# Where one projection of a dilated attention is computed: beside the values by block products, or in the attention's slots

## The chip, the cores and the metric

The kernel runs on one core of a Trainium2 chip. The metric is the device time of one execution in microseconds; the median of three runs is compared. One further execution was profiled, and the profile below is of that one.

## The reference

Two layers of a decoder on x of 1024 positions by 1024 features, in float32. Layer 0 mixes positions by a gated MLP, layer 1 by attention with three dilations; each is followed by a squared-ReLU MLP. The change touches the attention alone:

```python
B_PATTERNS = ((128, 1), (512, 4), (2048, 16))
def dilated_branch(q, k, v, window, dilation, slopes):
    span = window // dilation                                   # 128 in all three
    # positions in blocks of span x dilation; a query sees the keys of its own residue,
    # in its own block and in the one before
    s = jnp.einsum('bnqrhe,bnkrhe->bnrhqk', qb, kb) * (E ** -0.5)
    s = s + bias;  s = jnp.where(valid, s, NEG)                 # ALiBi, causal, within span
    m = jnp.max(s, axis=-1);  p = jnp.exp(s - m);  l = jnp.sum(p, axis=-1)
    o = jnp.einsum('bnrhqk,bnkrhe->bnqrhe', p / l, vb);  lse = m + jnp.log(l)
def mixer_b(h, w_qkv, w_out, slopes):
    qkv = (h @ w_qkv).reshape(B, S, N_PAT, 3, B_HEADS, B_HEAD_DIM)   # 16 heads of 64
    wts = softmax(lses over the patterns);  o = sum(wts * outs)
    return o.reshape(B, S, 1024) @ w_out
```

So nine projections of 1024 x 1024 (q, k and v for three dilations) come ahead of the attention proper.

## The kernel before

[...]

**The product stage** (`values`). v of all three dilations and q and k of dilation 1 are made by a scheme of seven products of half-size blocks in place of eight: `V_STEPS` lists (pattern g, X, product p) with X = 0 for q, 1 for k, 2 for v. A product has four blocks m of 128 rows; each is 12 matmuls 512 wide (`psv`, line 1283). `evict` takes the sums of a block out of PSUM: products 1, 5 and 6 are copied to `vpart`, the others add what was kept, split it into `vs` or `qs`, and GpSimd's queue stores that in DRAM (`v_dram`, `qk_dram`), 512 KB a block. Right-hand blocks of the weights come by `RightForms.load` (512 KB each) and are prepared two steps ahead.

**The attention stage** (`attention`). The 8 pairs of heads are taken in turn, and in each pair dilation 16, then 4, then 1 (`order`; g = 2, 1, 0). Each of these 24 units has 8 slots of two halves. `at(slot, half, rank)` and `in_half(half_slot, rank)` put pieces of work into a half slot; the loop at the end runs all half slots in order and puts projection steps between them. In a unit:

- `scores`: three matmuls a tile into `sc`, both heads at once (line 1473); `soften`: DVE adds the bias and takes the extreme (line 1493), ACT makes exponent and sum (line 1495), into `p`.
- `transposes` of `p` into `pT`; `halve` splits it into `pThi` (ACT) and `pTlo` (DVE); three half slots later `weighted` multiplies by v into `pv`, two banks of 512 positions.
- `gather`: for each of the two banks ACT copies one half of the sums into `oT` (line 1562) and DVE adds the other (line 1563).
- `merge`, for the three dilations of a pair: factors from the sums, and `scale`, `add`, `cut` on DVE (lines 1649 to 1653).

PSUM has two banks each for `sc`, `pv`, the transposes and the projections.

**Projections in the slots** (`project`). q and k of dilations 16 and 4, 8 pairs: 32 items of 128 columns, each two halves of 24 matmuls (`psq`, `psk`, line 1384), whose weights come by one load of 512 KB and are split (`wqk_hi`, `wqk_lo`). A step of the stream is 3 matmuls, so an item has 16 steps and there are 512. `lead` steps run ahead of the first half slot, the rest by a running credit:

```python
stream = project()
lead, credit = 7 * KD, 0
...
credit += 512 - lead
while credit >= 351:
    credit -= 351
    next(stream, None)
```

That is 1.3 steps a half slot, done after 351 of the 384. Blocks of q and k of dilation 1 are loaded by `load_block`, v by `load_v`, on SP's queue. The order on each engine is fixed when the kernel is built; a scheduler may move an instruction, above all a load, ahead of where the code stands. Near the end the slots also take the first part of the output product (`pso`, line 1756).

Of the kernel before, what the change touches and what calls it, by code (L numbers as in the profile page):

```python
# [10 lines left out]
F32 = mybir.dt.float32  # L11
# [6 lines left out]
P = 128  # L18
# [17 lines left out]
def trunk(ctx: ExitStack, tc: tile.TileContext, x, c, ada_w, ada_b, ln_g, ln_b, a_w_in, a_b_in,  # L36
# [1063 lines left out]
    qk_dram = dram.tile([N_PAIRS, 2, P, 2, S], F32, name="qk_0")  # L1100

# [43 lines left out]
    V_STEPS = [(g, X, p) for g, X in ((2, 2), (1, 2), (0, 2), (0, 0), (0, 1)) for p in (1, 2, 5, 6, 7, 4, 3)]  # L1145
# [11 lines left out]
    def values(before, right, ahead):  # L1157
# [3 lines left out]
        with ExitStack() as ph:  # L1161
# [79 lines left out]
            def evict(g, X, p, m):  # L1241
                acc = sums["pb" if p in (2, 5, 3) else "pa", m][:]
                if p in (1, 5, 6):
                    t = parts[p, m] = x_tile(f"vpart_{g}_{X}_{p}_{m}")
                    A.copy(t[:], acc)
                    return
                if p != 4:
                    t = parts.pop(({2: 1, 7: 5, 3: 6}[p], m))
                    V.tensor_tensor(t[:], acc, t[:], op=ALU.add)
                    acc = t[:]  # L1250
                half, dh = {2: (1, 0), 3: (1, 1), 4: (0, 0), 7: (0, 1)}[p]
                if X < 2:
                    t = parted.tile([P, 2, HALF], F32R, name=f"qs_{X}_{p}_{m}", tag="vs")
# [44 lines left out]
    def attention(form):  # L1298
# [5 lines left out]
        with ExitStack() as ph:  # L1304
# [104 lines left out]
            def attend(n, oT_of):  # L1409
# [21 lines left out]
                heads = [dict(probs={}, pvs=[], begun=[False, False]) for _ in range(2)]  # L1431
# [17 lines left out]
                if g == 0:  # L1449
                    for m, slot in enumerate((base - 4, base - 3, base + starts[0] + 1, base + starts[1] + 1)):  # L1450
                        at(slot, 0)(lambda m=m: load_block(m))

                def scores(m):
# [10 lines left out]
                    for t in groups[m]:  # L1464
# [4 lines left out]
                        tq, keys = slice(t * P - q_from, (t + 1) * P - q_from), slice(k0 - k_from, k0 - k_from + w)  # L1469
# [28 lines left out]
                for m, slot in enumerate(starts):  # L1498
                    at(base + slot, 0, 1)(lambda m=m: scores(m))
                    for part in range(2):  # L1500
                        at(base + slot, part, 3)(lambda m=m, part=part: soften(m, part))

                for e, st in enumerate(heads):
# [36 lines left out]
                    def weighted(m, e=e, h=h, rows=rows, packs=packs, pT=pT, pvs=pvs, st=st):  # L1540
                        if m == 0:
                            pvs.extend(bank("pv", f"pv_{h}_{g}_{b}") for b in range(2))
                        begun, left = st["begun"], st["left"]
                        for t, nxt, o in packs[m]:
                            stt = my["v"][:, t, 2 * e : 2 * e + 2, :].rearrange("p a c -> p (a c)")
                            for x_ in pT[m]:
# [3 lines left out]
                                for q0, o_, w_ in pieces:  # L1550
                                    b = q0 // HALF
                                    left[b] -= 1
# [4 lines left out]
                    def gather(e=e, rows=rows, pvs=pvs):  # L1557
# [298 lines left out]
```

## Time and profile before

| | |
|---|---|
| median of three runs | 2716.02 us (2713.87 to 2716.73) |
| profiled execution, its own time | 2714.54 us |
| its span, first to last instruction | 2712.8 us |
| mean granted clock of TensorE | 0.996 |
| product stage / ahead of the first score / slots up to the last projection | 386.3 / 38.4 / 539.3 us |
| last slots / output sums | 63.0 / 72.0 us |
| matmuls | 13242 |
| HBM read / written | 365.40 / 136.92 MB |

PE is TensorE's matmuls, PEld its weight loads, DVE VectorE, ACT ScalarE, POOL GpSimd, SP the engine that issues most transfers. A row of a group gives line, engine, operation, output<-input, shapes, count, then busy time and mean duration in ns, then the idle time of the engine just before and what ended it. A row of waits gives total, number of times and the longest. In the chain of waits a piece has its start, its length and what ran. Buffer numbers are left out of names, and lines are those of the kernel before.

### The profile page before, as it was taken

To read this page: it belongs to the slowest core of one execution; us is meant where nothing else is said; L and a number is where in the kernel's file an instruction comes from. 1 tells how busy PE (TensorE), PEld (TensorE's weight loads), DVE (VectorE), ACT (ScalarE), POOL (GpSimd) and SP (SyncE) were. 2 spreads that over 40 slices of the span, in tenths; PEclk is the share of its full clock that TensorE was granted. 3 is DMA by queue.
4 is the path that set the end of the run, shared out by engine and by line. 5 is a ranking of instruction groups with operands and counts; after the bars stand their busy time and mean duration, and the time that the engine had idled before them with its cause. 6 is when DMAs were issued, how large, how long until landed. Compare 5 with 4: busy or idle time off the path is not lost.

```text
span 2712.8 us, 37098 instructions
## 1 busy us (share of the span) xinstructions
PE 2652.8 (98%) x13242; PEld 2193.6 (81%) x13242; DVE 1993.4 (73%) x3610; ACT 1378.9 (51%) x2601; POOL 114.6 (4%) x193
## 2 busy tenths in 40 slices
PE   6999999999999999999999999999999999999998
PEld 5788888887888877888888888888877888878887
DVE  6787698877889778655647777777658966577877
ACT  3354375555444464443436666666645655554332
POOL 1000000000000001111111000000010000000000
PEclk9999999999999999999999999999999999999999
DMA  7534336667967745655475545554782654485562
GB/s 265 159 119 134 117 133 225 229 219 251 337 224 248 245 150 178 215 184 195 165 226 171 138 137 136 138 146 135 232 222 96 210 189 160 148 312 189 172 208 86
DMA packets 340781, 504.77 MB, mean 186 GB/s; under 512 B 51900, under 2 KB 177252, under 8 KB 340596
## 3 DMA queue, kind: packets, MB, share of 16 engines
q1 hardware_dynamic: 324212, 443.68, 51.4%
q0 software_dynamic: 16384, 58.73, 6.0%
q8 instruction: 104, 1.70, 0.3%
q14 instruction: 81, 0.66, 0.1%
HBM read 365.40 MB, written 136.92 MB: 185 GB/s over the span
## 4 chain that ended last, share of the span: by engine, by line
PE 82%; DVE 10%; DMA 4%; ACT 2%; issue 2%; SPq 0%; DVEq 0%; POOL 0%; ACTq 0%; POOLq 0%
PE psd L957 22%; PE psv L1283 13%; PE psua L798 9%; PE psk L1384 7%; PE psq L1384 7%; PE psuc L798 4%; PE pv L1553 3%; PE psd_wout L389 3%; PE psu L368 3%; PE sc L1473 3%; PE psub L798 2%; DMA adaw<-in_ada_w_dram 2%; PE psv L470 2%; PE pT L1526 1%; DVE left L103 1%
## 5 line engine op out<-in xcount | busy, mean ns | idle before, releaser
L798 PE MATMUL psua<-right,left 128*128 128x512 f32 x1536 | 363.2, 390 | 0.1
L957 PE MATMUL psd<-rhi,lhi 128*128 128x512 f32 x896 | 350.1, 391 | 3.0 <-ACT part L829 3.0
L957 PE MATMUL psd<-rlo,lhi 128*128 128x512 f32 x896 | 349.8, 390 | 0.2
L957 PE MATMUL psd<-rhi,llo 128*128 128x512 f32 x896 | 349.3, 390 | 0.0
L798 PEld LDWEIGHTS psua<-right,left 128*128 128x128 f32 x1536 | 287.3, 188 | 61.1 <-DVE right L103 1.2
L1495 ACT ACTIVATE p<-p,stat 128x128 f32<-128x128 f32 (+1 forms) x384 | 168.8, 441 | 95.4 <-DVE stat L1493 94.4
L957 PEld LDWEIGHTS psd<-rhi,lhi 128*128 128x128 f32 x896 | 168.6, 188 | 39.0 <-ACT part L829 3.9
L957 PEld LDWEIGHTS psd<-rlo,lhi 128*128 128x128 f32 x896 | 168.7, 188 | 35.7 <-DVE rlo L103 1.1
L957 PEld LDWEIGHTS psd<-rhi,llo 128*128 128x128 f32 x896 | 168.7, 188 | 35.0
L798 PE MATMUL psuc<-right,left 128*128 128x512 f32 x768 | 187.2, 391 | 0.0
L128 DVE SCALAR_TENSOR_TENSOR adaacc<-adaw,silu_c,adaacc 128x512 f32<-128x512 f32 x168 | 128.7, 776 | 55.7 <-DMA adaw<-in_ada_w_dram 55.0
L798 PEld LDWEIGHTS psuc<-right,left 128*128 128x128 f32 x768 | 143.6, 188 | 29.8 <-DVE right L103 0.2
L103 DVE TENSOR_TENSOR pTlo<-pT,pThi 128x512 fp32r<-128x512 f32 (+1 forms) x160 | 99.3, 621 | 76.0 <-ACT pThi L102 75.0
L103 DVE TENSOR_TENSOR left<-ws,left 128x512 fp32r<-128x512 f32 x128 | 88.0, 689 | 73.9 <-ACT left L102 72.0
L103 DVE TENSOR_TENSOR llo<-lraw,lhi 128x1024 fp32r<-128x1024 f32 x112 | 136.7, 1221 | 1.5 <-ACT lhi L102 1.5
L102 ACT CAST left<-ws 128x512 fp32r<-128x512 f32 x128 | 79.1, 620 | 98.3 <-DVE ws L719 88.5
L1384 PE MATMUL psk<-form_L,wqk_hi 128*128 128x512 f32 x384 | 127.0, 412 | 0.0
L1384 PE MATMUL psq<-form_L,wqk_hi 128*128 128x512 f32 x384 | 126.5, 410 | 0.0
L102 ACT CAST lhi<-lraw 128x1024 fp32r<-128x1024 f32 x112 | 117.2, 1047 | 9.3 <-PE psd L957 3.3
L1283 PE MATMUL psv<-vrhi,form_S 128*128 128x512 f32 x384 | 120.0, 391 | 0.8 <-ACT vrhi L102 0.5
L1493 DVE CUSTOM_DVE_ANT_0 p<-sc,bias 128x128 f32<-128x128 f32 (+1 forms) x384 | 113.7, 346 | 5.6 <-PE sc L1473 5.3
L102 ACT CAST pThi<-pT 128x512 fp32r<-128x512 f32 (+1 forms) x160 | 84.7, 529 | 62.1 <-PE pT L1526 45.3
(332 smaller groups left out, 6076.6 us busy)
## 6 DMA issues: line engine op xcount, KB each, us to landing
lraw<-forms SPq DMA_DIRECT2D x112, 512.0 KB
adaw<-in_ada_w_dram SPq DMA_DIRECT2D x192, 256.0 KB
up<-in_mlp_w_up_dram SPq DMA_DIRECT2D x64, 512.0 KB
forms<-s SPq DMA_DIRECT2D x128, 256.0 KB
rraw<-in_mlp_w_down_dram SPq DMA_DIRECT2D x64, 512.0 KB
forms<-part SPq DMA_DIRECT2D x96, 256.0 KB
v<-vs POOLq DMA_DIRECT2D x48, 512.0 KB, 3.9
vraw<-in_b_w_qkv_dram SPq DMA_DIRECT2D x42, 512.0 KB
```

The source lines that it names most:

```text
L102: first = A.copy(hi, src) if hi_engine is A else hi_engine.tensor_copy(hi, src)
L103: return first, lo_engine.tensor_tensor(lo, src, hi, op=ALU.subtract)
L128: ins = V.scalar_tensor_tensor(acc[:], raw[:], silu_c[:, k : k + 1], acc[:], ALU.mult, ALU.add)
L368: T.matmul(dst, s[a], m[b], start=(n == 0), stop=(n == last))
L389: T.matmul(p[:], stat[a][:, k, o : o + P], u[b][:, w], start=n == 0, stop=n == count - 1)
L798: T.matmul(acc, w[:, a, k, :], right[p][:, b, k, :], start=p in (1, 2, 5) and k + a + b == 0, stop=k == 3 and a == 1, skip_group_check=True)
L957: ins = T.matmul(sums[kind, m][:], l[a][:, k, m * P : (m + 1) * P], r[b][:, k, :], start=p in (1, 5, 2, 3) and kp + k + a + b == 0, stop=k ...
L1283: T.matmul(acc, rows[:, m * P : (m + 1) * P], cols_, start=p in (1, 2, 5) and kp + k + a + b == 0, stop=kp == 1 and k == 1 and a == 1, ski ...
L1384: T.matmul(p[:], wu[a][:, k * P : (k + 1) * P], h_op(k, half, b), start=k + c_ == 0, stop=k == KD - 1 and c_ == 2)
L1473: T.matmul(banks[e][:, sl], q_[a][rows, tq], k_[b][rows, keys], start=c_ == 0, stop=c_ == 2)
L1493: V.tensor_tensor_reduce(out=pr, in0=banks[e][:, sl], in1=st["bias"][:, width - w :], scale=-0.125, scalar=3e38, op0=ALU.add, op1=ALU.min, ...
L1495: A.activation(pr, pr, AF.Exp, bias=nm, scale=-1.0, accum_out=l)
```

## The change

Four things are changed.

- **q of dilation 4 moves.** `V_STEPS` gets the seven products of (1, 0), between v and the q of dilation 1. Its evictions read PSUM with a stride of 4, so that positions stand by residue, and store to `q1_dram`, one store of 512 KB a block. `project` has 24 items (384 steps) instead of 32; in its place `load_q` reads the two halves of a pair's q, 512 KB each, on SP's queue.
- **The lead and the pace.** 40 steps ahead instead of 56; then 328 steps over the first 326 half slots, and 16 over the rest up to 351.
- **Sums bank by bank.** `gather` copies a bank when its last product is done, and `join`, the add, stands a half slot later. A bank of `pv` is taken at its first use. The two row operations on `aff` stand a half slot apart, too.
- **Starts** are given in half slots, and the fourth of dilation 1 moves from 12 to 11.

```diff
-    V_STEPS = [(g, X, p) for g, X in ((2, 2), (1, 2), (0, 2), (0, 0), (0, 1)) for p in (1, 2, 5, 6, 7, 4, 3)]
+    V_STEPS = [(g, X, p) for g, X in ((2, 2), (1, 2), (0, 2), (1, 0), (0, 0), (0, 1)) for p in (1, 2, 5, 6, 7, 4, 3)]
...
+                def side(t):
+                    return t.rearrange("p (r i) -> p r i", r=4) if (g, X) == (1, 0) else t
+                if (g, X) == (1, 0):
+                    acc = acc.rearrange("p (i r) -> p r i", r=4)
...
-                    A.copy(t[:], acc)
+                    A.copy(side(t[:]), acc)
...
-                    V.tensor_tensor(t[:], acc, t[:], op=ALU.add)
+                    V.tensor_tensor(side(t[:]), acc, side(t[:]), op=ALU.add)
...
-                    split(t[:, 0], t[:, 1], acc)
-                    nc.gpsimd.dma_start(qk_dram[4 * dh + m, X, :, :, half * HALF : (half + 1) * HALF], t[:].bitcast(F32))
+                    split(side(t[:, 0]), side(t[:, 1]), acc)
+                    dst = q1_dram[4 * dh + m] if g else qk_dram[4 * dh + m, X]
+                    nc.gpsimd.dma_start(dst[:, :, half * HALF : (half + 1) * HALF], t[:].bitcast(F32))
...
-                todo = [(n, X) for n in range(len(order)) if order[n][1] for X in range(2)]
+                todo = [(n, X) for n in range(len(order)) for X in {0: (), 1: (1,), 2: (0, 1)}[order[n][1]]]
...
-                starts = {0: (0, 2, 3, 5) if last_one else (0, 2, 4, 6), 1: (0, 2, 5), 2: (0, 4)}[g]
+                starts = {0: (0, 4, 6, 10) if last_one else (0, 4, 8, 11), 1: (0, 4, 10), 2: (0, 8)}[g]
+                @at(max(0, base - 8), 0)
+                def load_q():
+                    if g != 1:
+                        return
+                    for i, m in enumerate(("qhi", "qlo")):
+                        my[m] = qk[1].tile([P, S], F32R, name=f"{m}_{hp}_1", tag=m)
+                        nc.sync.dma_start(my[m][:].bitcast(F32), q1_dram[hp, :, i, :])
...
-                        tq, keys = slice(t * P - q_from, (t + 1) * P - q_from), slice(k0 - k_from, k0 - k_from + w)
+                        q0 = (t % 2 * 4 + t // 2) * P if g == 1 else t * P - q_from
+                        tq, keys = slice(q0, q0 + P), slice(k0 - k_from, k0 - k_from + w)
...
-                        for b in range(2):
-                            dst = oT[rows, b * HALF : (b + 1) * HALF]
-                            A.copy(dst, pvs[b][rest, :])
-                            V.tensor_tensor(dst, dst, pvs[b][main, :], op=ALU.add)
+                    def gather(b, e=e, rows=rows, pvs=pvs, rest=rest):
+                        dst = oT_of(e, b)[rows, b * HALF : (b + 1) * HALF]
+                        A.copy(dst, pvs[b][rest, :])
+                    def join(b, e=e, rows=rows, pvs=pvs, main=main):
+                        dst = oT_of(1)[rows, b * HALF : (b + 1) * HALF]
+                        V.tensor_tensor(dst, dst, pvs[b][main, :], op=ALU.add)
...
-                    in_half(then + (not last_one), 2)(gather)
+                        for b in range(2):
+                            if m == ((1, 3) if g < 2 else (0, 1))[b]:
+                                done_at = then + (not last_one or b == 0)
+                                in_half(done_at, 2)(lambda b=b, f=gather: f(b))
+                                in_half(done_at + 1, 2)(lambda b=b, f=join: f(b))
...
-            lead, credit = 7 * KD, 0
+            lead, credit = 5 * KD, 0
...
-                    credit += 512 - lead
-                    while credit >= 351:
-                        credit -= 351
+                    credit += (368 - lead) * 25 if 2 * n + half_of < 326 else 16 * 326
+                    while credit >= 326 * 25:
+                        credit -= 326 * 25
```

What this does to the order of instructions is shown at three places. First PE, in the unit of dilation 16 of the fourth pair (heads 6 and 7), from the transposes of head 6's first pack (`pT_6_2_0`) to its first products with v (`pv_6_2_0`). Before:

```order
L1526 MATMUL pT_6_2_0_14644<-ident_73,p_6_2_0_14414 128x128 x2
L1526 MATMUL pT_6_2_0_14644<-ident_73,p_6_2_2_14431 128x128 x2
L1384 MATMUL psq_4_2_1_14633<-form_L11_8184,wqk_16_hi_14351 128x512 x2
L1384 MATMUL psq_4_2_1_14633<-form_L11_8184,wqk_16_lo_14352 128x512
L1384 MATMUL psq_4_2_1_14633<-form_L11_8184,wqk_16_hi_14351 128x512 x2
L1384 MATMUL psq_4_2_1_14633<-form_L11_8184,wqk_16_lo_14352 128x512
L1384 MATMUL psq_4_2_1_14633<-form_L12_8185,wqk_16_hi_14351 128x512 x2
L1384 MATMUL psq_4_2_1_14633<-form_L12_8185,wqk_16_lo_14352 128x512
L1384 MATMUL psq_4_2_1_14633<-form_L12_8185,wqk_16_hi_14351 128x512 x2
L1384 MATMUL psq_4_2_1_14633<-form_L12_8185,wqk_16_lo_14352 128x512
L1553 MATMUL pv_6_2_0_14672<-pThi_6_2_0_14653,v_3_2_14348 128x128
L1553 MATMUL pv_6_2_0_14672<-pTlo_6_2_0_14654,v_3_2_14348 128x128
```

The same place now:

```order
L1543 MATMUL pT_6_2_0_14953<-ident_73,p_6_2_0_14730 128x128 x2
L1543 MATMUL pT_6_2_0_14953<-ident_73,p_6_2_2_14753 128x128 x2
L1392 MATMUL psq_4_2_1_14912<-form_L12_8186,wqk_12_hi_14562 128x512 x2
L1392 MATMUL psq_4_2_1_14912<-form_L12_8186,wqk_12_lo_14563 128x512
L1392 MATMUL psq_4_2_1_14912<-form_L12_8186,wqk_12_hi_14562 128x512 x2
L1392 MATMUL psq_4_2_1_14912<-form_L12_8186,wqk_12_lo_14563 128x512
L1392 MATMUL psq_4_2_1_14912<-form_L12_8186,wqk_12_hi_14562 128x512 x2
L1392 MATMUL psq_4_2_1_14912<-form_L12_8186,wqk_12_lo_14563 128x512
L1570 MATMUL pv_6_2_0_14976<-pThi_6_2_0_14959,v_3_2_14671 128x128
L1570 MATMUL pv_6_2_0_14976<-pTlo_6_2_0_14960,v_3_2_14671 128x128
```

Nine projection matmuls stand between the transposes and their use, where twelve stood.

Second DVE at the same place, up to the low part of that pack (`pTlo_6_2_0`); `oT_2_0` are the sums of the pair before. Before:

```order
L103 TENSOR_TENSOR klo_3_1_14358<-psk_3_1_0_14491,khi_3_1_14357 128x4x128
L103 TENSOR_TENSOR wqk_19_lo_15058<-wk_4_1_raw_14629,wqk_19_hi_15057 128x1024
L1563 TENSOR_TENSOR oT_2_0_14482<-oT_2_0_14482,pv_5_0_1_14496 64x512
L103 TENSOR_TENSOR pTlo_6_2_0_14654<-pT_6_2_0_14644,pThi_6_2_0_14653 128x512
L1563 TENSOR_TENSOR oT_3_2_14785<-oT_3_2_14785,pv_6_2_0_14672 64x512
```

Now:

```order
L1649 RECIPROCAL mal_2_14893<-mal_2_14893 128x16
L1651 TENSOR_TENSOR ma_2_14888<-ma_2_14888,mal_2_14893 128x16 x3
L1582 TENSOR_TENSOR oT_2_0_14724<-oT_2_0_14724,pv_5_0_1_14831 64x512
L103 TENSOR_TENSOR pTlo_6_2_0_14960<-pT_6_2_0_14953,pThi_6_2_0_14959 128x512
L1582 TENSOR_TENSOR oT_3_2_15020<-oT_3_2_15020,pv_6_2_0_14976 64x512
```

The low parts of a key half and of a weight no longer stand ahead of `pTlo` there; small operations of `merge` do.

Third SP's queue, around the load of v for dilation 1 of the fifth pair (`v_4_0`); `mst` and `st_dram` carry the sums for `merge`, `bq` and `bk` are the blocks of dilation 1. Before:

```order
L1361 DMA wk_6_2_raw_16041<-in_b_w_qkv_dram 128x8x128
L1608 DMA mst_4_16348<-st_dram_11367 128x4x8
L1361 DMA wq_6_1_raw_16302<-in_b_w_qkv_dram 128x8x128
L1423 DMA v_4_0_15908<-v_0_108 128x8x256
L1588 DMA st_dram_11367<-stat_4_1_15633 128x8x4
L1608 DMA mst_4_16348<-st_dram_11367 128x4x8
L1441 DMA bq_4_2_15984<-qk_0_111 128x2x256
L1441 DMA bk_4_2_15986<-qk_0_111 128x2x384
```

Now:

```order
L1369 DMA wq_7_2_raw_16620<-in_b_w_qkv_dram 128x8x128
L1450 DMA qhi_5_1_16520<-q_1_112 128x1024
L1450 DMA qlo_5_1_16522<-q_1_112 128x1024
L1431 DMA v_4_0_16145<-v_0_108 128x8x256
L1611 DMA st_dram_11900<-stat_4_1_15887 128x8x4
L1631 DMA mst_4_16566<-st_dram_11900 128x4x8
L1457 DMA bq_4_2_16224<-qk_0_111 128x2x256
L1457 DMA bk_4_2_16226<-qk_0_111 128x2x384
```

The two loads of the next pair's q stand ahead of `v_4_0` and of the blocks, where the weight of q of dilation 4 stood.

More of the change, by code (lines that the diff above doesn't have):

```diff
@@ L1100, in trunk @@
     qk_dram = dram.tile([N_PAIRS, 2, P, 2, S], F32, name="qk_0")
+    q1_dram = dram.tile([N_PAIRS, P, 2, S], F32, name="q_1")
     class RightForms:
@@ L1551, in weighted @@
                                     b = q0 // HALF
+                                    if b not in pvs:
+                                        pvs[b] = bank("pv", f"pv_{h}_{g}_{b}")
                                     left[b] -= 1
```

35 lines of the change are left out of this document (16 added, 19 removed).

## The prediction

> **What bounds the kernel now.** I read the page first, then the table of windows over the stages that the change touches, the chain of waits there, and PE's waits. The page: PE is busy in 98% of the span, and PE matmuls make 82% of the chain that ends last.
>
> ```profile
> PE 2652.8 (98%) x13242; PEld 2193.6 (81%) x13242; DVE 1993.4 (73%) x3610; ACT 1378.9 (51%) x2601; POOL 114.6 (4%) x193
> PE 82%; DVE 10%; DMA 4%; ACT 2%; issue 2%; SPq 0%; DVEq 0%; POOL 0%; ACTq 0%; POOLq 0%
> ```
>
> Windows of the five stages in order: block products, projections ahead of the first score, slots up to the last projection, last slots, and the output sums (columns: length, PE, weight load, DVE, ACT, POOL, clock, DMA share, GB/s).
>
> ```profile
> 991.00:1377.30 386.30, 385.46 (x1714) 317.98 (x1713) 248.03 (x310) 171.28 (x244) 47.49 (x80) 1.00 0.57 197
> 1377.30:1415.70 38.40, 38.40 (x172) 31.54 (x170) 15.46 (x18) 10.12 (x14) 3.35 (x7) 1.00 0.75 232
> 1415.70:1955.00 539.30, 539.06 (x3650) 454.36 (x3651) 387.18 (x1190) 344.87 (x1034) 23.85 (x51) 1.00 0.53 149
> 1955.00:2018.00 63.00, 60.62 (x392) 50.42 (x391) 38.24 (x115) 41.06 (x113) 8.21 (x10) 1.00 0.93 238
> 2018.00:2090.00 72.00, 66.38 (x297) 53.56 (x297) 54.02 (x132) 27.90 (x43) 0.00 (x0) 0.95 0.41 130
> ```
>
> In the first three PE has no hole, and DVE (64%, 40%, 72%) and ACT have room. A full row of PE could hide waits, since matmuls overlap. So I take their price from the chain of waits in order of time (start, length, what, count):
>
> ```profile
> 1224.89 152.77 PE psv L1283 x674
> 1388.54 10.88 PE psk L1384 x48
> ...
> 1493.43 1.39 PE psk L1384 x6
> ...
> 1499.13 1.57 PE psq L1384 x6
> ...
> 1504.16 2.78 PE psq L1384 x12
> ```
>
> 152.77/674 and 10.88/48 are both 0.227 us per 512-wide matmul back to back. In the slots a run of 6 takes 1.39 and one of 12 takes 2.78, 0.232 each; behind a score burst the run of 6 takes 1.57, so a handover costs up to 0.18.
>
> [...] Priced by weight load (2193.6/13242 = 0.166 us each), the 48 matmuls that the change saves would be worth 8 us, against 11 by the chain's pitch.
>
> PE's weight loads waited in the slots (waits view, 1415 to 1930 us: total, times, longest):
>
> ```profile
> PEld sc L1473 <- issue: 9.0, 53, 0.4
> PEld pv L1553 <- DVE pTlo L103: 1.0, 4, 0.3
> PEld pT L1529 <- ACT p L1495: 0.7, 2, 0.4
> ```
>
> The first row is a cost of each score burst and stays. The others are the real waits for DVE and ACT, under 2 us in 515. PE's own work sets the time.
>
> **The change part by part.** The tile view of `psq`, PE alone, gives the projections of q, half of them for dilation 4:
>
> ```profile
> L1384 PE MATMUL psq<-form_L,wqk_hi x384: 387/393/506, 1377.5 to 1935.4; 128*128 128x512 f32 x192
> L1384 PE MATMUL psq<-form_L,wqk_lo x192: 387/393/401, 1378.0 to 1935.6; 128*128 128x512 f32 x192
> L1384 PE MATMUL psq<-form_S,wqk_hi x128: 387/393/502, 1382.9 to 1929.6; 128*128 128x512 f32 x128
> L1384 PE MATMUL psq<-form_S,wqk_lo x64: 389/393/398, 1383.4 to 1929.8; 128*128 128x512 f32 x64
> ```
>
> *Matmuls.* They sum to 768; 384 go. Seven products of 4 blocks with 12 matmuls each come: 336. Beside the values: 336 x 0.227 = +76.2 us. Ahead of the first score: the lead falls from 56 to 40 steps of 3, so 48 x 0.227 = -10.9. In the slots 336 go: -77.9 at 0.232. The instruction lists hold 284 projection runs between first score and last projection before and 278 after, so nearly all handovers stay: 6 x 0.18 = -1. Sum: **-13.6**. Bounds: if a slot matmul is worth no more than 0.227, -11.2 without the runs; if it is worth the mean of the two runs of 6 above, (1.39 + 1.57)/12 = 0.247, -17.7. I take 0.232, because runs of 6 and 12 give the same.
>
> *What the products bring beside PE.* Each product has the weight cuts, evictions and 512 KB stores that the products of q and k of dilation 1 have now, written to other rows of the tile. Their stretch is the first chain row: no hole in 152.77 us, although ACT there waits for landings (waits, 985 to 1385):
>
> ```profile
> ACT qs L102 <- DMA qk<-qs: 31.0, 14, 5.0
> ```
>
> 16 more stores add about 16 us of such waits, beside ACT's 171 of 386; I cost them at nothing. Without the cover, 0 to 16. The strided read of PSUM moves from the projection's cut to the eviction; if it were dearer there, DVE's 36% of room takes it.
>
> *Two queues.* The projection's weights of q (8 loads of 512 KB) become 12, and 16 loads of q itself come on SP's queue. Per pair of heads that is 0.5 MB more net in the slots: at 149 GB/s for a share of 0.53, full rate is 281, so 1.8 us of transfer; the share rises from 0.53 to about 0.62. In SP's order the two loads of q stand ahead of v and of the third and fourth q and k blocks of dilation 1, some 4 us of transfer in front of blocks wanted half a pattern later. Nothing. If the cover is gone it shows at the end, below.
>
> *Sums bank by bank.* The add waits half a slot behind ACT's copy, so DVE doesn't stand for it. Each bank is copied when its last product is done: the first frees earlier, the second's add comes half a slot later than now. The lists of DVE and ACT over one pair in the steady part (waits behind the bar):
>
> ```profile
> L103 DVE TENSOR_TENSOR pTlo<-pT,pThi 128x384 fp32r<-128x384 f32 (+1 forms) x20 | 12.4, 622 | 10.8 <-ACT pThi L102 10.5
> L1563 DVE TENSOR_TENSOR oT<-oT,pv 64x512 f32<-64x512 f32 x12 | 8.2, 684 | 5.3 <-ACT oT L1562 5.2
> ...
> L103 DVE TENSOR_TENSOR wqk_lo<-wq_raw,wqk_hi 128x1024 fp32r<-128x1024 f32 x3 | 3.7, 1225 | 0.8 <-ACT wqk_hi L102 0.6
> ...
> L103 DVE TENSOR_TENSOR qlo<-psq,qhi 128x512 fp32r<-128x512 f32 x3 | 2.1, 692 | 1.7 <-ACT qhi L102 1.7
> L102 ACT CAST pThi<-pT 128x384 fp32r<-128x384 f32 (+1 forms) x20 | 10.6, 528 | 8.0 <-PE pT L1526 5.7 <-PE pT L1529 2.1
> ```
>
> And the same pair's three patterns by windows:
>
> ```profile
> 1633.60:1657.60 24.00, 24.00 (x167) 20.43 (x166) 15.94 (x60) 14.37 (x47) 0.77 (x2) 1.00 0.29 79
> 1657.60:1681.80 24.20, 24.20 (x165) 20.43 (x163) 18.14 (x52) 15.38 (x46) 0.81 (x2) 1.00 0.59 131
> 1681.80:1707.70 25.90, 25.90 (x175) 21.54 (x174) 19.94 (x55) 18.81 (x51) 0.59 (x2) 1.00 0.64 199
> ```
>
> DVE works 54.0 of 74.1 us. It loses two `qlo` and one `wqk_lo`, 2.6, leaving 51.4; PE loses 42 x 0.232 = 9.7, leaving 64.4. DVE goes from 73 to 80%, with 13.0 us of room for what are now 20.1 us of waits. The 5.3 for `oT` should mostly go; of the 10.8 for `pTlo`, ACT itself waits 7.8 for PE's transposes, and that shrinks with PE. So DVE still fits, but with less cover.
>
> *New PE waits.* The tightest place is the first pack of dilation 16 (timeline):
>
> ```profile
> 1652.13 0.60 PE L1526 MATMUL pT<-ident,p 128*128 128x128 f32 x4
> 1652.81 1.22 DVE L103 TENSOR_TENSOR wqk_lo<-wk_raw,wqk_hi 128x1024 fp32r<-128x1024 f32 x1 [0.26 <-ACT wqk_hi L102]
> 1654.79 0.69 DVE L103 TENSOR_TENSOR pTlo<-pT,pThi 128x512 fp32r<-128x512 f32 x1
> 1655.54 0.19 PEld L1553 LDWEIGHTS pv<-pTlo,v 128*128 128x128 f32 x1 [0.23 <-DVE pTlo L103]
> ```
>
> Twelve projection matmuls cover transpose to use; nine will, 0.7 us less. If DVE came as late as here, 0.7 more in 8 pairs, 5.6 us. After, the `wqk_lo` of 1.22 no longer stands ahead of `pTlo` there, so it may be nothing. Other packs lose about as much cover but have more. I take 4 between 0 and 8.
>
> Total: -13.6 + 4 = **-9.6, say -9**. The profiled execution took 2714.5 (span 2712.8); the median of the runs is 1.5 above it. So 2705.5 for such an execution, and 2707 for the median. About 0.2%, 5.4 us, is what a measurement can tell from no change.
>
> **The rivals.**
>
> *Late transfers at the end* (0.17). In the last pair's first two patterns the DMA engines are full, and PE has waited for a block once:
>
> ```profile
> 1954.20:1980.50 26.30, 26.30 (x173) 22.15 (x172) 18.34 (x53) 16.33 (x50) 3.14 (x4) 1.00 1.03 300
> PE sc L1473 <- DMA bk<-qk: 1.3, 1, 1.3
> ```
>
> The pattern ahead of this window loses 30 projections, 7 us, of the time in which the same output weights and rows must land. For: the share of 1.03. Against: SP's new order issues some of these loads earlier. It gives back up to 7: -13.6 + 4 + 7 = -3, **2713**, no change.
>
> *DVE sets the pace* (0.13). In-order waits keep their length while the half slots shrink by a seventh. DVE's work and waits then set a pair: 51.4 + w against PE's 64.4. Slower by 5.4 needs 8 x (w - 13.0) above 19, so w above 15.4. For: without `oT` 14.8 of today's 20.1 are left, close to that. Against: 7.8 of these hang on PE itself. Halfway between 13.0 and 20.1, w = 16.5: 8 x 3.5 = +28, in place of the 4: -13.6 + 28 = +14, **2730**; all 20.1 would give +43.
>
> *Cheaper slots* (0.12). A removed slot matmul is worth 0.247 and nothing new waits: -17.7, **2698**.
>
> *The clock* (0.03). It was granted at 1.00 in the slots and 0.95 in the output sums, where PE stood idle 5.6 of 72 us: 0.05 x 72 = 3.6 us lost. If a late q or block holds PE some 4 us in one place, 4 + 3.6 beyond the sum give -2, **2714**. [...]
>
> That the change does not do what it says cannot be: the lists hold 48 matmuls fewer.
>
> **How the numbers follow.** The forecast has 0.55: PE stays the bound with 0 to 8 us of new waits, 2703 to 2711 around 2707. Its upper end touches the bound of 0.2%, so 0.50 of it counts as faster; with the cheaper slots 0.62. Slower: 0.13. The rest, 0.25, is within 0.2%. The range, 2697 to 2723, takes in cheaper slots, late transfers and the clock, and half the way to a pace by DVE; what is left out is most of DVE's 0.13 and a few hundredths below.
>
> **What would show it.** Right: seven products more at about 10.9 us each, the first score about 27 us behind the last product instead of 38, a steady pair of 64 to 66 us instead of 74, and PE's waits for `pTlo` in the slots below 8 us. Wrong: pairs of 67 us or more with DVE without idle time, PE waiting for `bk` or output weights at the end, or a clock below 1.00 in the slots. A product stage over 465 us would mean that its stores no longer hide.

## The result and the profile after

The changed kernel took 2724.9 us (median of 6 runs, 2721.8 to 2728.8) against 2716.2 for the kernel before: ratio 1.0036, 95% interval 1.0023 to 1.0049. It is slower by 0.36%, where 0.3% faster was forecast. The profiled execution's span went from 2712.8 to 2723.0.

The same five stages of the changed kernel, by windows (length, PE, weight load, DVE, ACT, POOL, clock, DMA share, GB/s):

```profile
990.00:1452.70 462.70, 461.54 (x2049) 381.09 (x2048) 291.86 (x360) 201.29 (x286) 57.84 (x96) 1.00 0.56 195
1452.70:1481.80 29.10, 27.79 (x122) 22.45 (x120) 10.68 (x14) 8.00 (x11) 3.25 (x6) 1.00 0.94 292
1481.80:1964.50 482.70, 468.70 (x3304) 391.52 (x3303) 370.20 (x1170) 328.91 (x1012) 25.44 (x52) 1.00 0.62 179
1964.50:2030.00 65.50, 64.40 (x401) 53.65 (x401) 39.18 (x115) 41.70 (x114) 8.19 (x10) 0.95 0.86 209
2030.00:2102.00 72.00, 66.37 (x297) 53.58 (x296) 54.28 (x133) 27.92 (x43) 0.00 (x0) 0.95 0.41 137
```

Against before the products took +76.4, the lead -9.3, the slots **-56.6**, the last slots +2.5 and the output sums 0; outside of these 2.8 went, 1.0 of it ahead of the products. The forecast for the slots was -77.9 - 1 + 4 = -74.9: all but a little of the miss is there. PE, which had no hole in the slots (539.06 of 539.30), now has 14.0 us of them.

What PE's weight loads waited for in lead and slots (waits view, 1452 to 1965 us: total, times, longest):

```profile
PEld sc L1490 <- issue: 8.9, 52, 0.4
PEld pv L1570 <- DVE pTlo L103: 8.7, 17, 0.7
PEld pv L1570 <- ACT pThi L102: 7.4, 11, 1.7
PEld sc L1490 <- DVE stat L1510: 6.2, 12, 1.0
PEld sc L1490 <- DVE aff L1726: 1.9, 2, 1.6
PEld psk L1392 <- DVE qlo L103: 1.7, 1, 1.7
```

The issue row is as before. Of the others, `psk` belongs to the lead; the rest, with two smaller rows of 0.8 and 0.2, are 25.2 us of waits in the slots. Before, such rows came to 3.7 us: the 1.7 of the two that the prediction shows, and 2.0 in six small ones that it leaves out. In the second to the sixth pair they come again at up to three places. The timeline at the first, the first pack of dilation 16:

```profile
1697.97 0.39 ACT L1512 ACTIVATE p<-p,stat 128x128 f32<-128x128 f32 x1
...
1698.48 0.58 ACT L1578 COPY oT<-pv 64x512 f32<-64x512 f32 x1
...
1699.08 0.59 ACT L102 CAST pThi<-pT 128x512 fp32r<-128x512 f32 x1
1699.09 0.69 DVE L1582 TENSOR_TENSOR oT<-oT,pv 64x512 f32<-64x512 f32 x1 [0.23 <-ACT oT L1578]
...
1699.72 0.19 PEld L1570 LDWEIGHTS pv<-pThi,v 128*128 128x128 f32 x1 [0.33 <-ACT pThi L102]
...
1699.81 0.69 DVE L103 TENSOR_TENSOR pTlo<-pT,pThi 128x512 fp32r<-128x512 f32 x1
...
1700.55 0.19 PEld L1570 LDWEIGHTS pv<-pTlo,v 128*128 128x128 f32 x1 [0.65 <-DVE pTlo L103]
```

ACT finishes the exponentials of the last burst and the previous pattern's copy of `oT` before it comes to `pThi`; DVE does the join before `pTlo`. PE has run through its nine projection matmuls and waits 0.33 and then 0.65. The second place is the second pack of dilation 4, with the same order ahead of it (waits of 0.79 and 0.62 in the pair before this one, 0.46 and 0.62 in this one). The third is the fourth score burst of dilation 1, moved from half slot 12 to 11, whose bank DVE has not read out yet (1.05 in the pair before). A steady pair takes 66.5 to 67.9 us from one such place to the next, not 74.1 and not the 64.4 of the forecast. One pair by windows:

```profile
1635.00:1702.70 67.70, 65.50 (x462) 54.74 (x461) 51.50 (x163) 46.11 (x141) 2.50 (x6) 1.00 0.59 163
```

DVE's groups in it (waits behind the bar), and ACT's:

```profile
L103 DVE TENSOR_TENSOR pTlo<-pT,pThi 128x512 fp32r<-128x512 f32 (+1 forms) x20 | 12.4, 620 | 6.6 <-ACT pThi L102 6.6
L1582 DVE TENSOR_TENSOR oT<-oT,pv 64x512 f32<-64x512 f32 x13 | 8.9, 684 | 8.7 <-ACT oT L1578 8.7
```

```profile
L1512 ACT ACTIVATE p<-p,stat 128x128 f32<-128x128 f32 (+1 forms) x48 | 21.1, 441 | 13.8 <-DVE stat L1510 13.8
L102 ACT CAST pThi<-pT 128x512 fp32r<-128x512 f32 (+1 forms) x20 | 10.4, 527 | 2.9 <-PE pT L1546 1.9 <-PE pT L1543 0.9
```

DVE's 51.5 us of work is what was forecast (51.4). Its wait for `oT` rose from 5.3 to 8.7, and ACT's wait for PE's transposes shrank from 8.0 to 2.9: ACT and DVE wait less for PE than before, and PE waits for them.

### The profile page after: what moved, and what is told of

It is laid out like the page before. It is cut to its first block, busy times and chain, and to the rows that moved or that the text cites. A ratio compares the mean times of both kernels' runs of the same rounds, so it can differ in the third digit from the quotient of the medians.

```text
span 2723.0 us, 37136 instructions
## 1 busy us (share of the span) xinstructions
PE 2650.2 (97%) x13194; PEld 2187.8 (80%) x13194; DVE 2015.6 (74%) x3636; ACT 1391.2 (51%) x2619; POOL 126.5 (5%) x209
## 4 chain that ended last, share of the span: by engine, by line
PE 47%; issue 26%; DVE 15%; DMA 5%; ACT 4%; POOL 3%; SPq 0%; POOLq 0%; DVEq 0%; ACTq 0%
PE psd L957 11%; PE psua L798 8%; PE psuc L798 4%; PE psk L1392 3%; PE psd_wout L389 3%; PE psu L368 3%; DMA adaw<-in_ada_w_dram 2%; PE psq L1392 2%; PE pv L1570 2%; PE sc L1490 2%; PE psv L470 2%; PE psub L798 2%; ACT p L1512 1%; DVE adaacc L128 1%; DVE pTlo L103 1%
## 5 line engine op out<-in xcount | busy, mean ns | idle before, releaser
L1291 PE MATMUL psv<-form_S,vrhi 128*128 128x512 f32 x384 | 118.3, 389 | 0.0
L102 ACT CAST rhi<-rraw 128x1024 fp32r<-128x1024 f32 x48 | 50.5, 1052 | 117.3 <-issue 78.8
```

What stands on the lines that cost most here:

```text
L102: first = A.copy(hi, src) if hi_engine is A else hi_engine.tensor_copy(hi, src)
L1291: T.matmul(acc, rows[:, m * P : (m + 1) * P], cols_, start=p in (1, 2, 5) and kp + k + a + b == 0, stop=kp == 1 and k == 1 and a == 1, ski ...
```

## The experiments

**Theory at the start.** By PE's own work the half slot is a seventh shorter, the latency from transposes to `pTlo` is not. PE's work between the two is called cover: packs that were just covered now wait. Rivals: the gather bank by bank or the order of single instructions causes the waits; VectorE's work (51.5 of 67.7 us) sets the pair. *Waits* below is the sum of the rows of PE's weight loads as above, without issue, 1482 to 1964 us (25.2 in the changed kernel, 2.7 before; the kernel before has more slots ahead of this stretch); *slots* is the time from the first score to the first score of the last pair's dilation 4 (482.6, and 538.5 before).

**Is it lost cover?** The padded kernel puts the removed matmuls back as pure PE work.

```diff
+                    if g == 1:      # behind each half of k's projection
+                        p = bank("mm", f"psd_{hp}_{half}")
+                        for k in range(KD):   # the same three matmuls again, then yield
...
-            lead, credit = 5 * KD, 0
+            lead, credit = 7 * KD, 0
```

> The changed kernel with the 384 matmuls of dilation 4's q put back into the slots as PE work alone (into a bank that nobody reads, same weights, no eviction), lead and pace of the kernel before. Nothing else differs from the changed kernel. Theory (the waits are the loss of PE work that covered ScalarE and VectorE): the 384 matmuls, worth 384 x 0.232 = 89 us, cost only 62 to 70 us, time 2787 to 2795, and PE's waits for pThi, pTlo and the score banks in the slots fall from 22 to below 4 us. Rival (the waits come from the gather or the order of instructions, whatever PE's cover): they stay at 18 to 25 us and the time is 2811 to 2816.

2794.4 us (2791.2 to 2796.5). The slots by windows:

```profile
1494.00:2032.30 538.30, 537.10 (x3642) 453.96 (x3641) 372.12 (x1169) 329.32 (x1011) 25.40 (x52) 1.00 0.56 159
```

The three largest waits in them that are not issue:

```profile
PEld sc L1497 <- DVE aff L1733: 1.3, 2, 1.0
PEld pv L1577 <- DVE pTlo L103: 0.7, 1, 0.7
PEld sc L1497 <- DVE bc L1683: 0.5, 3, 0.2
```

The waits are gone (3.6 in all), and the slots last as long as before the change. 336 more matmuls cost 538.3 - 482.7 = 55.6 us, 0.165 each, not 0.232. The theory holds: taking matmuls out of these slots pays only 70%, and the rest turns into waits. Gather, starts and the new loads are all in this kernel and cost nothing while PE covers them.

**Is it the gather, or the order at one place?** Three edits.

```diff
# e3: the gather of the kernel before
-            in_half(done_at, 2)(lambda b=b, f=gather: f(b)); in_half(done_at + 1, 2)(lambda b=b, f=join: f(b))
+            in_half(then + (not last_one), 2)(gather)      # both banks, copy and add adjacent
# e1: copy and join pinned behind pThi and pTlo of their half slot
-            A.copy(dst, pvs[b][rest, :])
+            tc.keep_in_program_order(A.copy(dst, pvs[b][rest, :]))     # the join likewise, rank 2.5
# e2
-            (0, 4, 8, 11), 1:
+            (0, 4, 8, 12), 1:
```

> The changed kernel with the gather as it was before: both banks at the end of the last pack, copy and add of a bank one after the other; q of dilation 4 stays in the product stage, pace and starts stay as changed. Theory (the waits come from the shorter half slot, not from the gather): same waits, 2724 to 2728, so the gather bank by bank is worth 0 to 3 us. Rival (the late join is what makes VectorE wait 8.7 us a pair for oT and holds pTlo back): the time falls by 8 to 15 us, to 2710 to 2717.

2730.6 us (2726.7 to 2735.0), ratio to before 1.0049 (1.0036 to 1.0063); waits 23.1. Going back to the old gather removes nothing, so the new one did not bring the waits (e4 has it too, and hardly any waits). The test is a mild one: the scheduler and not the written order decides, and the profile of e3 has at the first place the same order, the copy ahead of `pThi` and the join ahead of `pTlo`, with the same waits of 0.33 and 0.65. The interval overlaps that of the changed kernel, so whether its gather bank by bank wins a few us stays open.

> The changed kernel with each gather's copy (ScalarE) and join (VectorE) issued behind the pThi and pTlo of the same half slot, held there in the issue order. Theory (PE's new waits come from work that stands ahead of pThi and pTlo, at the first pack of dilation 16 and the second of dilation 4): PE's waits for pThi and pTlo in the slots (7.4 and 8.7 us in the changed kernel) fall by 8 to 12 us together, the time goes from 2724.9 to 2713 to 2718. Rival (VectorE's work of 51.5 us a pair sets the pace, in whatever order it stands): the waits only move to other places, time within 3 us of 2724.9.

2733.9 us (2730.1 to 2739.0): slower, as neither theory had it. PE's largest waits other than issue, 1482 to 1965 us:

```profile
PEld sc L1490 <- DVE stat L1510: 7.9, 9, 1.7
PEld pv L1570 <- ACT pThi L102: 4.1, 6, 1.7
PEld pv L1570 <- DVE pTlo L103: 3.7, 8, 0.7
```

The waits for `pThi` and `pTlo` fell to half, as the order theory wanted, but those for the score banks grew from 6.2 to 7.9. Waits are 18.3 in all, 7 less, and yet the slots take 485.5. One reason is the clock, which comes up below: here it was granted at 0.75 to 0.77 in three stretches of 6.8 us of the slots. Why the work behind the attention took 4 us longer in this execution stays open.

> The changed kernel with the fourth score burst of dilation 1 back at half slot 12 (11 in the changed kernel). Theory: the 6.2 us that PE waits for a score bank (sc waits for DVE stat) fall to 1 or less, time 2718 to 2721. Rival (VectorE is late there by its load, so the next consumer waits in its place): the waits reappear at pThi/pTlo of dilation 1 or of the next pattern, time 2724 to 2728.

2725.2 us (2722.0 to 2728.7): no change. The waits that changed (1482 to 1964 us):

```profile
PEld pT L1546 <- ACT p L1512: 5.5, 7, 1.3
...
PEld sc L1490 <- DVE stat L1510: 0.7, 4, 0.2
```

The wait for the bank (6.2) is gone, and its whole length stands at the transposes of the third pack, which need the fourth burst's exponentials two half slots after it. A wait taken away came back one step later. The rival had the time and the return, but at another step (`pThi` or `pTlo`).

**Is it VectorE's load?** The merge's multiplications and sums were left out in the slots; first all ten, with the merge's last step moving ahead (e5), then the four sums (e6), then all ten again with the last step written at its old half slot (e9).

```diff
# e5, behind the last pair's list
+                pieces = ((cut, 0),)
# e6
+                pieces = ((scale, 2), (scale, 1), (scale, 0), (cut, 0))
# e9
-                pieces = ((scale, 2), (scale, 1), (scale, 0), (add, 2), (add, 1), (cut, 0))
+                none = lambda g, half: None
+                pieces = ((none, 2), (none, 1), (none, 0), (none, 2), (none, 1), (cut, 0))
```

> The changed kernel without the merge's multiplications and sums in the slots of pairs 0 to 6 (10 VectorE instructions of a pair: 6 x 0.949 + 4 x 0.684 = 8.4 us of VectorE's 51.5); the weights go on in place of the merged outputs, PE's work is the same. Theory as it now stands (VectorE and ScalarE hand each other work in turn, and a pair is VectorE's work plus its waits for ScalarE): the steady pair falls from 67.5 to PE's own 64 to 65 us, slots 482.7 to 460 to 467, time 2703 to 2710. Rival (PE waits at fixed places because 9 matmuls cover less than the latency of pThi and pTlo): waits stay, pair 66.5 to 67.5, time 2718 to 2725.

2734.9 us (2728.2 to 2737.0). This edit made a new wait: the last step's copy on ACT now waits for the weights' transfer, with exponentials behind it, 1.6 to 2.9 us in each of six pairs and 14.0 in all. So it can't judge the load.

> A third of that dose: only the four sums of the merge are left out (4 x 0.684 = 2.7 us of VectorE a pair). Theory (VectorE's work sets the pair): 67.5 falls by 1.5 to 2.7 us, slots to 464 to 473, time 2709 to 2717. Rival (fixed latency): 0 to 0.5 us a pair, time 2721 to 2726.

2724.9 us (2720.5 to 2726.8), waits 25.4, slots 482.4: 2.7 us less of VectorE's work a pair changed nothing, where the load theory had 464 to 473 us of slots. ACT's copy of the merge's last step waits some 0.8 us a pair in this run, 4.6 in all, less than the 10 to 19 us that this theory expected to win.

> As the run without the merge's multiplications and sums (8.4 us of VectorE's 51.5 a pair), but every other step of the merge stays at its half slot (in the first try the last step moved ahead and its copy on ScalarE waited for the weights). Load theory (VectorE's work sets the pair): pair 67.5 falls to 64 to 65, time 2703 to 2710. Fixed latency theory (pThi and pTlo come later than 9 matmuls cover where exponentials and a copy of oT stand ahead of them on ScalarE): the wait at the first pack of dilation 16 stays as it is (about 0.9 us a pair), the one at the second pack of dilation 4 shrinks, since two multiplications stand among the reductions ahead of it; pair 65.5 to 67, time 2712 to 2721.

2730.2 us (2724.8 to 2735.5), waits 25.6, slots 483.7. The same stretch of a pair as above, by windows:

```profile
1635.00:1702.70 67.70, 65.45 (x461) 54.64 (x460) 44.13 (x152) 45.55 (x140) 2.49 (x6) 1.00 0.58 163
```

DVE's groups in it:

```profile
L103 DVE TENSOR_TENSOR pTlo<-pT,pThi 128x512 fp32r<-128x512 f32 (+1 forms) x20 | 12.2, 620 | 8.3 <-ACT pThi L102 8.2
L1582 DVE TENSOR_TENSOR oT<-oT,pv 64x512 f32<-64x512 f32 x12 | 8.2, 686 | 12.3 <-ACT oT L1578 12.3
```

DVE has 7.4 us less to do and PE's 65.45 busy of 67.7 has not moved: DVE waits longer, 12.3 for `oT` in place of 8.7. But the wait of e5 is here as well. The scheduler moved the last step ahead all the same, in this pair from 1669.84 us to 1644.35, and its copy waits for the weights with exponentials behind it, again 14.0 us in six pairs (ACT alone, timeline):

```profile
1644.35 0.62 ACT L102 CAST bc<-bc 128x512 fp32r<-128x512 f32 x1 [2.01 <-DMA bc<-w_dram]
```

So the time of e9 can't settle the question either, and this wait is one reason why it is 5 us slower than the changed kernel. Its places do tell something. The waits at the first place stay (0.32 and 0.65), those at the second fall from 1.4 to 0.5, those of the fourth burst go, and 1.3 to 2.1 us a pair come new at the last pack of dilation 16, behind this copy. What stands in DVE's queue at a place therefore counts. That its load as a whole does not set the pair rests on e6, on the 16 us of a pair in which DVE stands idle, and on e7, e11 and e18 below, where no engine has less to do and the slots get shorter by up to 8.4 us. A sum of the form "work plus waits" fits any pair, since the waits fill what is left. No run takes work off ACT, so ACT's load is not tested in the same way; it is busy for 46.1 us of the 67.7.

**Can the waits be removed where they stand?** Cover moved to the two packs (e7), one more half slot of lag for them (e8), exponentials moved ahead of them (e10), this with e2's start (e11).

```diff
# e7: 1.5 times the steps at half slots 12 to 14, half at 0, 4 and 8
-                    credit += (368 - lead) * 25 if ...
+                    credit += (368 - lead) * (25 + {0: -12, 4: -12, 8: -12, 12: 12, 13: 12, 14: 12}.get((2 * n + half_of) % 16, 0) * (n < 160)) if ...
# e8
-                            then = half_slot + 3
+                            then = half_slot + 3 + (e == 0 and (g, m) in ((2, 0), (1, 1)))
# e10; e11 has 12 for 11 in dilation 1 as well
-                1: (0, 4, 10), 2: (0, 8)}[g]
+                1: (0, 4, 8), 2: (0, 6)}[g]
```

> The changed kernel with its projection steps spread differently over the 16 half slots of a pattern, the same number in all: half as many at half slots 0, 4 and 8 (where score bursts stand), one and a half times as many at 12, 13 and 14 (13.5 matmuls of cover in place of 9 ahead of the first pack of dilation 16 and the second of dilation 4). No engine has more or less work. Fixed latency: the waits for pThi and pTlo in the slots fall from 16 to below 6 us and the time to 2712 to 2718. VectorE's work as the pace: PE waits elsewhere for as long, time 2722 to 2728.

2719.5 us (2716.3 to 2724.4), ratio 1.0017 (1.0009 to 1.0025); waits 18.4. Between the two theories: cover without any work won 5 us.

> The changed kernel with pv of just two packs a pair and pattern (the first pack of dilation 16 and the second of dilation 4, first head) one half slot later: 12 matmuls of cover ahead of them. Fixed latency: these two places stop waiting (1.0 + 1.4 us a pair), time 2712 to 2719. VectorE's work as the pace: the waits turn up behind, time 2722 to 2727.

2730.0 us (2724.9 to 2731.2). The waits fell to 18.7, the slots rose to 487.5. Windows at one place of five successive pairs show where that went (the clock is the third number from the end):

```profile
1604.80:1611.60 6.80, 5.73 (x30) 4.60 (x30) 6.39 (x22) 6.10 (x19) 0.91 (x2) 0.75 0.80 227
...
1740.80:1747.60 6.80, 5.33 (x28) 4.22 (x27) 6.51 (x22) 5.09 (x16) 0.52 (x2) 0.75 0.87 269
...
1876.80:1883.60 6.80, 5.31 (x30) 4.30 (x28) 6.51 (x21) 5.52 (x17) 0.91 (x2) 0.79 0.92 272
```

The timeline of the second pair, which the list leaves out, PE alone:

```profile
1670.61 0.67 PE L1392 MATMUL psk<-form_L,wqk_hi 128*128 128x512 f32 x2
...
1673.03 0.39 PE L1570 MATMUL pv<-pTlo,v 128*128 128x256 f32 x1 [0.26 <-DVE pTlo L103]
...
1674.65 1.32 PE L1490 MATMUL sc<-bk,bq 64*128 64x256 f32 x12 [1.07 <-DVE stat L1510]
1675.90 1.22 PE L1392 MATMUL psk<-form_L,wqk_hi 128*128 128x512 f32 x2
...
1679.87 0.63 PE L1392 MATMUL psk<-form_L,wqk_hi 128*128 128x512 f32 x2
```

Two waits of 0.26 and 1.07 within 2 us, and then the pair of matmuls takes 1.22 in place of 0.67; over the 6.8 us from 1672.80 the granted clock was 0.75. Each such stretch loses 1.4 to 1.7 us (6.8 us at 0.79 to 0.75) beyond the wait itself, some 8 in five pairs.

> The changed kernel with the last score burst of dilation 16 at half slot 6 in place of 8 and that of dilation 4 at 8 in place of 10; dilation 1 as changed, no work added or left out. Fixed latency theory: the exponentials are done when pThi comes, so PE's waits for pThi and pTlo at these two packs (7.4 and 8.7 us in all in the slots) fall below 6 us together; time 2709 to 2717. Load theory: time 2722 to 2728.

2720.5 us (2714.2 to 2725.7), ratio 1.0018 (1.0007 to 1.0029); waits 20.7, of which 13.9 are for `pThi` and `pTlo`, not below 6. The wait for `pThi` at the first pack of dilation 16 is gone, that for `pTlo` is short; the first pack of dilation 4 and the last of dilation 1 wait in their place, behind the moved exponentials.

> The same two earlier bursts, and the fourth burst of dilation 1 back at half slot 12. Fixed latency theory: 2706 to 2716, below the changed kernel by 9 or more and at or below the kernel before. Load theory: 2722 to 2728.

2719.5 us (2713.8 to 2722.0), ratio 1.0011 (1.0002 to 1.0020), waits 23.0. Five us below the changed kernel, not nine.

**Do they move on for good?** Steps dealt out by pack (e12), the burst of dilation 4 at 7 (e13), both (e15), the kernel before with the earlier bursts (e14), another spacing of dilation 1's bursts (e16), and a mild dealing out with that (e17) and with e11 (e18).

```diff
# e12 on e11, e15 on e13: weights of the 48 half slots of a pair in place of 25
+            PACE: 38 at 8-10 and 12-14 of dilation 16 and 8-14 of dilation 4, 22 at 2-4 of dilation 16, 20 elsewhere
# e13 on e11
-                1: (0, 4, 8), 2: (0, 6)}[g]
+                1: (0, 4, 7), 2: (0, 6)}[g]
# e14 on the kernel before (whole slots)
-                1: (0, 2, 5), 2: (0, 4)}[g]
+                1: (0, 2, 4), 2: (0, 3)}[g]
# e16 on e10
-                (0, 4, 8, 11), 1:
+                (0, 3, 7, 11), 1:
# e17 on e16, e18 on e11
-                    credit += (368 - lead) * 25 if ...
+                    credit += (368 - lead) * (25 if n >= 160 else 29 if 8 <= (2 * n + half_of) % 16 < 15 else 22) if ...
```

> The kernel with the earlier bursts and the fourth burst of dilation 1 at 12 (2719.5), with its projection steps dealt out by pack: 1.5 times as many at the half slots ahead of the packs that still wait there (8 to 10 and 12 to 14 of dilation 16, 8 to 14 of dilation 4), 0.8 times elsewhere, the same number in all. Latency theory (each pack's pv waits by what its pThi and pTlo are later than its cover): PE's waits for pThi and pTlo in the slots fall from 13.6 to below 6 us, time 2709 to 2715, below the kernel before. Rival (the waits move on with the cover): 2717 to 2722.

> The same without the dealing out, third burst of dilation 4 at half slot 7 in place of 8: its exponentials are done before the first pack's pThi, which waited 2.6 us for ScalarE in the version with 8. Latency theory: the first pack of dilation 4 waits no more (some 0.4 us a pair), the score burst itself may wait for its bank; time 2714 to 2720. Rival: 2719 to 2724.

> The kernel before, with the same earlier bursts (dilation 16 at 6, dilation 4 at 8), nothing else. PE waits there for only 3.3 us in all slots, so by the latency theory there is next to nothing to win: 2712 to 2718. Rival (the earlier bursts are better by themselves, for a reason that has nothing to do with cover): 2706 to 2711, as much won as in the changed kernel (5 us).

> Burst at 7 and the dealing out by pack together. Latency theory: 2706 to 2714, PE's waits for pThi and pTlo in the slots below 5 us. Rival: 2717 to 2722.

> The earlier bursts of dilation 16 and 4 (as in the run at 2720.5), and dilation 1's bursts at half slots 0, 3, 7 and 11 in place of 0, 4, 8 and 11, so that four half slots in place of three lie between its third burst and its fourth. Theory (each wait is one step's latency against its own cover): PE's waits for the score banks (5.7 us in the slots) fall below 2, none comes at pT; time 2714 to 2719. Rival (a wait that is removed turns up at the next step): 2719 to 2725.

> The same with the projection steps dealt out a little: 29 parts at half slots 8 to 14 of each pattern, where most waits are, 22 at the others (25 before). Theory: the short waits there (23 of 0.4 us for pTlo, 10 for pThi) fall by half, time 2709 to 2716. Rival: 2718 to 2725.

> The version at 2719.5 (earlier bursts, fourth burst of dilation 1 at 12) with the same mild dealing out. Theory: 2712 to 2718. Rival: 2718 to 2724.

| run | us, median (range) | ratio to before (95%) | waits | slots |
|---|---|---|---|---|
| changed kernel | 2724.9 (2721.8 to 2728.8) | 1.0036 (1.0023 to 1.0049) | 25.2 | 482.6 |
| e12 paced by pack | 2722.8 (2720.3 to 2727.3) | 1.0030 (1.0019 to 1.0042) | 20.9 | 478.5 |
| e13 burst at 7 | 2725.5 (2723.6 to 2732.2) | 1.0043 (1.0031 to 1.0055) | 26.3 | 483.4 |
| e14 before, early bursts | 2716.5 (2712.6 to 2721.4) | 1.0001 (0.9991 to 1.0010) | 4.3 | 540.3 |
| e15 both | 2733.0 (2728.3 to 2740.0) | 1.0070 (1.0057 to 1.0083) | 25.9 | 482.4 |
| e16 bursts 0, 3, 7, 11 | 2726.8 (2719.6 to 2727.7) | 1.0037 (1.0023 to 1.0051) | 21.9 | 480.8 |
| e17 with mild pace | 2722.4 (2715.8 to 2726.0) | 1.0024 (1.0014 to 1.0034) | 20.2 | 479.4 |
| e18 e11 with mild pace | 2718.1 (2714.0 to 2722.6) | 1.0007 (0.9995 to 1.0019) | 16.6 | 474.2 |

e14 is as the latency theory had it: where PE covers, the earlier bursts win nothing. Of the other six only e18 comes near what that theory expected, at the edge of both ranges. e17 fell into the rival's range; e12, e13 and e16 came out 1 to 2 us above it and e15 11 us, slower than either theory had it. In e12 the waits for `pThi` and `pTlo` fell from 13.6 to 8.2, not below 6, and others grew (1482 to 1965 us):

```profile
PEld pT L1546 <- ACT p L1512: 7.2, 7, 1.6
PEld pv L1570 <- DVE pTlo L103: 5.5, 16, 0.5
PEld pv L1570 <- ACT pThi L102: 2.7, 4, 0.9
PEld sc L1490 <- DVE pTlo L103: 2.4, 3, 2.1
```

e13 moved the long waits to `pThi` (11.2). e16 took the bank waits away (0.6 in place of 5.7) and has 20.6 at `pThi` and `pTlo`. Of these only e18 has clearly less in sum, though its wait at `pT` is 3.6 where the changed kernel has 0.2 (1482 to 1965 us):

```profile
PEld pv L1570 <- DVE pTlo L103: 7.0, 19, 0.6
PEld pT L1546 <- ACT p L1512: 3.6, 6, 1.3
PEld pv L1570 <- ACT pThi L102: 3.5, 6, 0.8
```

Its waits are 8.6 us less than the changed kernel's, its slots 8.4 and its time 6.8. It is the best version with q among the products, and not to be told from the kernel before. No version with q among the products beat the kernel before.

## Why the prediction was wrong

- *Product stage, +76.2:* right. It took +76.4 with 462.7 in all; the 16 more stores stayed hidden (PE busy for 461.5 of it) and the clock was 1.00.
- *Lead, -10.9:* -9.3. The difference is for the most part one wait of a projection for `qlo`, which the lead did not have before (1.7 us for its weight load; PE stood idle 1.3).
- *Slots, -77.9:* the pitch of 0.232 was not refuted; the cover was mispriced. With 21.5 us more of waits than before (25.2 against 3.7), -77.9 - 1 + 21.5 gives -57.4, and -56.6 was measured.
- ***New PE waits*, 4 between 0 and 8:** this step failed. They came to 25.2, against 3.7 before. The prediction's "under 2 us" had read two rows of eight. The tightest place had been found, but the remark that without the 1.22 us `wqk_lo` it "may be nothing" left out what else stands ahead: exponentials and the copy of `oT` on ACT, the join on DVE (the timeline above; waits 0.33 and 0.65 there). And "other packs lose about as much cover but have more" counted the loss from the transposes on, three matmuls or 0.7 us. The second pack of dilation 4, the dearest place now, shows what that misses. Before, its low part ended 1.1 us ahead of its weight load at 1680.24 (fourth pair, timeline):

```profile
1678.55 0.56 DVE L103 TENSOR_TENSOR pTlo<-pT,pThi 128x384 fp32r<-128x384 f32 x1
```

But its chain begins at the score burst ahead of it, with the exponentials that hold ACT up. From that burst's first matmul to the pack's first weight load PE took 7.9 us before and takes 6.5 now, without its wait there; from the same matmul to the end of the low part it was 7.0 us and is 7.7. That is 2.1 us of reserve lost where 1.1 were there. The slots gave -56.6 where -74.9 was forecast, 18 us short of it (22.3 in place of the 4), and the forecast missed by 17.9. Padding them again showed that it is cover (e4).
- *"The 5.3 for `oT` should mostly go":* wrong; it rose to 8.7, and the order at the first place is the same with the old gather (e3).
- *Rival, DVE sets the pace (2730, w above 15.4):* w was 67.7 - 51.5 = 16.2 and the time 5 us from its number, but its mechanism fell. DVE stands idle for those 16.2 us, 2.7 us less of its work a pair changed nothing (e6), and moving cover or bursts about, with the same work, made the slots shorter (e7, e11, e18). That the number was near is luck. Latency at single steps, through ACT and DVE in turn, is what remains.
- *Rival, late transfers at the end:* fell. PE waited for a block once, and in the first pair (PE's waits, 1482 to 1550 us); the last slots show no wait for a DMA.

```profile
PE sc L1490 <- DMA bk<-qk: 1.4, 1, 1.4
```

- *Rival, the clock (0.03):* it did come, in the last pair, and not for a block of 4 us. Windows there:

```profile
1961.00:1964.50 3.50, 2.34 (x17) 1.50 (x15) 2.41 (x7) 2.02 (x6) 0.07 (x1) 1.00 0.67 201
1964.50:1967.90 3.40, 3.40 (x22) 3.09 (x22) 2.43 (x11) 1.79 (x7) 0.00 (x0) 0.50 0.82 244
1967.90:1971.30 3.40, 3.40 (x9) 2.63 (x9) 0.49 (x6) 1.84 (x9) 0.00 (x0) 0.50 1.03 235
```

PE was idle for 3.50 - 2.34 = 1.2 us, and the clock was granted at 0.50 for the next 6.8, a loss of 3.4: more than the +2.5 of the last slots. The hold of some 4 us that this rival supposed came nowhere: PE's longest wait in the slots and the last slots was 1.4 us, the one for `bk` above.
- *Cheaper slots:* the opposite; a matmul taken out of them was worth 56.6/336 = 0.168.

## What to carry over

Work taken off the bottleneck engine is worth its full time only where nothing needs it as cover (in these slots a matmul paid 0.165 us of its pitch of 0.232, e4). Before pricing it, list for every step that other engines feed the time from its input to its use against the work of the bottleneck between them, with everything that stands ahead of it in the feeding engines' queues; before the change, that list would have shown the first pack of dilation 16 with no reserve (0.23 us of wait already), and the second of dilation 4, counted from its score burst, with 1.1 us of reserve where 1.4 of PE's work go. Where several such chains run through the same two engines, a wait removed at one place tends to stand at the next: judge an edit by the sum of the waits, and by the clock.

## What the hardware showed beyond that

Behind short waits TensorE's clock was granted below 1.00. In e8, at one place of five successive pairs, it was 0.75 to 0.79 over 6.8 us in which PE was idle for 1.1 to 1.5; in the second of these pairs the two waits were 0.26 and 1.07 us, within 2 us. In the changed kernel 1.2 us of idle time in 3.5 stood ahead of 6.8 us at 0.50. One wait of PE's weight load in its first pair was longer, 1.7 us for `pThi` (PE itself waited 1.3), and the clock was 1.00 there and behind it:

```profile
1490.00:1497.00 7.00, 6.09 (x37) 4.70 (x33) 6.96 (x23) 3.87 (x18) 2.19 (x3) 1.00 0.61 215
1497.00:1500.00 3.00, 2.25 (x14) 1.80 (x15) 2.58 (x3) 0.94 (x3) 2.03 (x3) 1.00 0.37 120
1500.00:1503.50 3.50, 3.50 (x30) 2.92 (x29) 2.91 (x15) 2.51 (x9) 0.00 (x0) 1.00 0.42 135
```

So in these runs the length of a wait did not by itself tell whether the clock fell; what decides it was not shown. The five stretches of e8 stand at the same place of a pair, in windows 68.0 us apart, and so are not five independent cases.

The same matmul has three prices in this kernel: 0.227 us added among the products, 0.232 by its pitch in a run of the slots, and 0.165 to 0.168 when it is put back into them (e4) or taken out.
